# Where the row factor of the first RMSNorm is applied, how the first loads are queued, and where three transposes stand

## The chip, the cores and the metric

The kernel runs on one core of a Trainium2 chip. The time is the device time of one execution in microseconds (us). The kernel before took 1512.64, 1515.22 and 1515.03 us in three timed runs; their median is 1515.03 us. A fourth run was recorded by the hardware profiler and took 1514.31 us, of which 1512.5 us lie between its first and its last instruction. That part is called the span; 1.81 us lie around it.

Five engines work side by side, each through its own queue of instructions: PE multiplies matrices (PEld, which loads its stationary operand, runs beside it), DVE, ACT and POOL do elementwise work, and SP here only issues transfers. ACT and POOL issue some transfers too.

## The reference, cut to what matters

One layer over 256 tokens of width 2048, all in fp32:

```
u = x * rsqrt(mean(x*x) + eps) * g1           # RMSNorm
z = u @ W_in   -> stick-breaking q/k/v | forgetting q/k/v + forget logits
                  | RWKV-7 r/k/v and three low-rank inputs | 3 gates of 2048
y_A, y_B: attention (4 heads x 128 each);  y_C: RWKV-7 (16 heads x 64)
rwkv:  z = z + (z_prev - z) * mu              # shift by one token
m = sum_i sigmoid(gate_i) * (y_i @ P_i);  x = x + RMSNorm(m @ W_out)
x = x + RMSNorm(relu(RMSNorm(x) @ W_up)^2 @ W_down)
```

The factor rsqrt(...) is one number per token (a row of u), and every product with W_in is linear in u.

## The kernel before, in words

**Products.** An fp32 product is made of three faster ones. An operand is split into a high part, rounded by ACT to the matmul's format, and the rest, which DVE subtracts. Weights come from one stream of blocks of 128 x 1024 fp32 (512 KB), in the order of use, into tiles `raw` of which there are three (`wraw`, L145, issued on SP). ACT makes `whi` (L152) and DVE makes `wlo` (L153), three tiles of each; splits are made one block ahead. x or u is kept turned (features on partitions, tokens along the row) as 16 tiles of 128 x 512: 256 columns of high parts, then 256 of low parts. For a unit of 128 output columns PE multiplies whi with all 512 columns (L168, L176) and wlo with the 256 high ones (L172), eight tiles of u per block. `evac` adds the two halves of the PSUM bank (ACT copies one at L224, DVE adds at L225). A second form, `tok`, makes 256 tokens x 512 columns with u as the stationary operand (L198, L214); it serves the values of both attentions and the gates.

**Order of the work.** PE runs in the order in which its instructions are written (`manual_schedule`); on the other engines a list scheduler sets the order. The attentions and the RWKV part (`mixers`, in it `rwkv_half` for each half of the heads) and `gate_norm` are generators. They are advanced between matmuls by a virtual clock: `tick` adds 0.227 us for a matmul, `yield 3.0` holds the generator for 3.0 us of that clock, `yield "k3"` waits until `mark("k3")` is 2.6 us old (`SETTLE`).

**The begin** (L260 to L313). ACT issues the parameters and x in four pieces (L260, L263); SP issues the blocks 0, 2 and 4, then the constants. ACT and DVE split x*g1 into `xpk` (L233, L234). The first three units share the first loads: for features 0 to 7, matmuls of all three units follow as tiles arrive (L308, L310), then the products with wlo (L313); then the same for features 8 to 15 with blocks 1, 3 and 5. The fourth unit begins at L168.

**The row factor.** During unit 4, `norm` squares x, sums over features on PE (L329) and makes `rstd`, the factor per token along the row. The eight stick-breaking q and k units are made from x*g1 and scaled by DVE at L349. For everything after them, `normed` makes u = x*g1*rstd (DVE L338), splits it again (ACT L230, DVE L231) and fills the 16 tiles `upk`.

**Shift.** `shift` serves 24 r, k and v units and three low-rank inputs: ACT copies half of the bank (L525), DVE adds (L526), ACT scales by mu into a tile shifted by one token (L527), DVE combines (L528).

**The triangular inverse** in `rwkv_half` is built in `Ti` by small DVE operations (L734, L736). Then DVE turns it by a transpose into `TW` (L740) and by two into `SC` (L744), with a `yield` behind each, and PE multiplies these.

## Time and profile before

| What | Value |
|---|---|
| timed runs | 1512.64, 1515.22, 1515.03 us, median 1515.03 |
| profiled run, its span | 1514.31 us, 1512.5 us |
| PE busy | 1479.7 us, 98% |
| DVE busy | 1213.7 us, 80% |
| ACT busy | 938.4 us, 62% |
| POOL busy | 86.1 us, 6% |
| from the start to the first matmul | 8.88 us |
| first matmul of the fourth unit | 29.23 us |
| bytes moved | 317.70 MB, 210 GB/s over the span |

A row of the timeline begins with start and duration in us; then come the engine, the line of the source, the operation, the tile written, the tiles read, shapes, and the count where equal neighbours are shown as one row. The bracket at the end holds the time for which the engine had stood idle, and what released it. In the view by windows each engine has its busy us in the stretch and, in brackets, its number of instructions; the last three columns are the granted clock of PE (1.00 is full), the share of the transfer engines and GB/s. "q" behind an engine's name (SPq, ACTq) is its queue, where it issues transfers.

### The profile page before, as it was taken

How to read it: one execution, taken by the hardware profiler on the slowest of the kernel's cores; microseconds unless marked ns; L12 is line 12 of the kernel's file. 1: busy time of each engine (PE TensorE's matmuls, PEld its weight loads, DVE VectorE, ACT ScalarE, POOL GpSimd, SP SyncE). 2: the span in 40 equal slices, each digit the busy share in tenths (PEclk: the TensorE clock that was granted, in tenths of full speed). 3: DMA queues.
4: the chain of work that ended last, by engine and by line, in shares of the span. 5: the costliest groups of instructions: out<-in, count | busy, mean ns of one | idle time of the engine just before them, and what ended most of it. 6: DMA issues, size and time to landing. Idle time of an engine off the chain costs nothing.

```text
span 1512.5 us, 22758 instructions
## 1 busy us (share of the span) xinstructions
PE 1479.7 (98%) x8387; PEld 1247.3 (82%) x8387; DVE 1213.7 (80%) x1675; ACT 938.4 (62%) x1408; POOL 86.1 (6%) x159
## 2 busy tenths in 40 slices
PE   7999999999999999999999999999999999999997
PEld 6888888887777887788887888888888888888885
DVE  6876677789669799567656788999899999899996
ACT  7665666654566554565444767777677676677662
POOL 0011000100001100000000000000000000000000
PEclk9999999999999999999999999999999999999999
DMA  7555445545544445445784668888879788889884
GB/s 260 184 180 171 164 168 183 172 155 194 182 146 153 166 168 180 160 147 196 252 293 159 219 207 244 245 245 264 265 234 270 243 248 253 254 249 274 251 258 150
DMA packets 107039, 317.70 MB, mean 210 GB/s; under 512 B 10672, under 2 KB 14640, under 8 KB 106544
## 3 DMA queue, kind: packets, MB, share of 16 engines
q1 hardware_dynamic: 93536, 282.76, 54.5%
q0 software_dynamic: 8064, 29.36, 10.4%
q10 hardware_dynamic: 5328, 4.13, 0.8%
q8 instruction: 66, 1.08, 0.3%
q14 instruction: 45, 0.37, 0.1%
HBM read 282.65 MB, written 4.19 MB: 190 GB/s over the span
## 4 chain that ended last, share of the span: by engine, by line
PE 49%; issue 3%; DMA 3%; DVE 1%; ACT 0%; POOL 0%; POOLq 0%; DVEq 0%; ACTq 0%
PE gps L168 13%; PE gps L214 10%; PE gps L172 7%; PE gps L198 3%; PE mps L1324 3%; PE mps L1326 3%; PE mps L1325 3%; PE gps L1326 2%; PE gps L1324 2%; PE gps L1325 2%; PE gps L176 1%; DMA raw<-in_wst_dram 1%; DMA raw<-raw 1%; DMA sp<-raw 1%; DMA sp<-in_wst_dram 1%
## 5 line engine op out<-in xcount | busy, mean ns | idle before, releaser
L153 DVE TENSOR_TENSOR wlo<-raw,whi 128x1024 fp32r<-128x1024 f32 x507 | 616.6, 1225 | 169.4 <-ACT whi L152 155.7
L152 ACT ACTIVATE whi<-raw 128x1024 fp32r<-128x1024 f32 x507 | 532.9, 1056 | 257.1 <-DMA raw<-in_wst_dram 89.8
L168 PE MATMUL gps<-pk,whi 128*128 128x512 f32 x1301 | 330.5, 393 | 0.2 <-DVE pk L1116 0.2
L214 PE MATMUL gps<-whi,pk 128*128 128x512 f32 x1144 | 289.4, 392 | 0.0
L168 PEld LDWEIGHTS gps<-pk,whi 128*128 128x128 f32 x1301 | 241.7, 189 | 47.7 <-DVE pk L1116 0.6
L214 PEld LDWEIGHTS gps<-whi,pk 128*128 128x128 f32 x1144 | 212.7, 188 | 44.2
L172 PEld LDWEIGHTS gps<-pk,wlo 128*128 128x128 f32 x1391 | 189.9, 190 | 13.4 <-DVE wlo L153 0.2
L172 PE MATMUL gps<-pk,wlo 128*128 128x256 f32 x1391 | 195.5, 283 | 0.0
L214 PE MATMUL gps<-wlo,pk 128*128 128x512 f32 x572 | 155.6, 392 | 3.1 <-DVE wlo L153 3.1
L214 PEld LDWEIGHTS gps<-wlo,pk 128*128 128x128 f32 x572 | 106.2, 188 | 26.0 <-DVE wlo L153 3.9
L1190 DVE TENSOR_TENSOR sp<-raw,sp 128x1024 fp32r<-128x1024 f32 x67 | 81.9, 1223 | 6.6 <-ACT sp L1189 6.4
L1189 ACT ACTIVATE sp<-raw 128x1024 fp32r<-128x1024 f32 x67 | 70.5, 1053 | 15.3 <-DMA raw<-in_wst_dram 5.1
L1216 ACT ACTIVATE sp<-gps 128x512 f32<-128x512 f32 x52 | 31.0, 597 | 68.6 <-PE gps L176 68.5
L198 PE MATMUL gps<-whi,pk 128*128 128x512 f32 x264 | 72.3, 396 | 1.1 <-ACT whi L152 1.1
L1324 PE MATMUL mps<-whi,fm 128*128 128x512 f32 x168 | 66.2, 394 | 0.0
L1325 PE MATMUL mps<-whi,fm 128*128 128x512 f32 x168 | 65.9, 392 | 0.0
L1326 PE MATMUL mps<-wlo,fm 128*128 128x512 f32 x168 | 65.6, 391 | 0.0
L198 PEld LDWEIGHTS gps<-whi,pk 128*128 128x128 f32 x264 | 49.6, 190 | 12.2 <-ACT whi L152 1.8
L1286 POOL DMA_DIRECT2D raw<-raw x40 | 34.9, 873 | 428.4 <-DVE raw L1283 132.7
L1326 PE MATMUL gps<-wlo,fm 128*128 128x512 f32 x126 | 49.3, 391 | 0.4 <-DVE wlo L153 0.4
L1324 PE MATMUL gps<-whi,fm 128*128 128x512 f32 x126 | 49.3, 391 | 0.0
L1283 DVE TENSOR_TENSOR raw<-raw,raw 128x1024 f32<-128x1024 f32 x40 | 48.9, 1223 | 0.4
(383 smaller groups left out, 1984.3 us busy)
## 6 DMA issues: line engine op xcount, KB each, us to landing
raw<-in_wst_dram SPq DMA_DIRECT2D x502, 512.0 KB, 4.4
raw<-raw POOLq DMA_DIRECT2D x40, 512.0 KB, 7.5
sp<-in_wst_dram SPq DMA_DIRECT2D x16, 512.0 KB, 6.0
raw<-sp POOLq DMA_DIRECT2D x8, 512.0 KB, 7.3
sp<-raw POOLq DMA_DIRECT2D x8, 512.0 KB, 7.5
x<-in_x_dram SPq DMA_DIRECT2D x8, 256.0 KB, 6.4
xs<-x SPq DMA_DIRECT2D x2, 1024.0 KB, 4.1
x<-xs SPq DMA_DIRECT2D x4, 512.0 KB, 6.0
```

Source lines behind the costliest of these rows:

```text
L152: A.activation(hi, raw, AF.Copy)
L153: V.tensor_tensor(lo, raw, hi.bitcast(F32), ALU.subtract)
L168: PE.matmul(ps, hi[:, i * 128:i * 128 + 128], pks[i], start=first and i == 0, stop=False)
L172: PE.matmul(ps[:, 0:T], lo[:, i * 128:i * 128 + 128], pks[i][:, 0:T], start=False, stop=False)
L198: PE.matmul(ps[tt], pks[k][:, c:c + 128], w[:, (k - k0) * 512:(k - k0) * 512 + 512], start=k == 0 and part == 0 and w is hl[0], stop=w is ...
L214: PE.matmul(ps[tt], pks[k][:, c:c + 128], w[:, (k - k0) * 512:(k - k0) * 512 + 512], start=k == 0 and part == 0 and w is hl[0], stop=False)
L1189: A.activation(hi, raw, AF.Copy)
L1190: V.tensor_tensor(lo, raw, hi.bitcast(F32), ALU.subtract)
L1283: V.tensor_tensor(x, x, z, ALU.add)
L1324: PE.matmul(Q[f], p, w, start=d == 0 and i == 0, stop=False)
L1325: PE.matmul(Q[f], pl, w, start=False, stop=False)
L1326: PE.matmul(Q[f], p, wl, start=False, stop=d == nd - 1 and i == 1)
```

## The change

It has three parts.

1. **Row factor.** `normed` is gone. The 16 tiles of x*g1 that the begin makes serve all units. The factor is applied where a PSUM bank is emptied: POOL multiplies a 128 x 256 tile by `rstd` (`scaled`) for the 16 q and k units of both attentions and within the 27 shifts, between their DVE addition and ACT's scaling. Where tokens lie on partitions (`tok`), the factor goes in as the per-partition scale of the ACT instruction that empties the bank anyway: in `vtok`, and, halved, in the Tanh of the gates. `turned_rstd` makes that column form: two small matmuls turn four rows of the mean square, DVE copies, POOL raises to the power -0.5, DVE halves.
2. **Begin.** All first loads are issued on SP, in an order by need and in halves of a block. PE gets five matmuls of zeros with nothing to wait for but a memset. PE does features 0 to 3 for the three units, then 4 to 7, then 8 to 15 unit by unit. Block 1 and the last quarter of x are issued behind the other first loads; block 1 waits there for the tile `raw` of block 0. Squares are held in program order on ACT.
3. **Transposes.** `pin` (keep_in_program_order) holds the transposes into `U`, `TW` and `SC`, and a few ACT instructions, in their written place among their engine's instructions; two holds of the clock grow from 3.0 to 3.7. The tile `lor` shares the place of another one (`zx`).

The diff, cut to its core:

```diff
+    def pin(ins):
+        return tc.keep_in_program_order(ins)
...
+    zt = rp.tile([128, T], F32, tag="tha", name="zt", bufs=1)
+    V.memset(zt, 0.0)
+    idle = mps()
+    for i in range(5):
+        PE.matmul(idle[:, 0:T], zt[:, 0:128], zt, start=True, stop=True)
+    nc.sync.dma_start(out=par, in_=params)
     raws = {}
-    for a, b, n in ((0, 2, 0), (2, 4, 2), (4, 8, 4), (8, 16, 1)):
-        nc.scalar.dma_start(out=X0[:, a:b, :], in_=xt[:, a:b, :])
-        raws[n] = wraw(n)
+    def load(n, q=None):
+        if n not in raws:
+            raws[n] = wpool.tile([128, HALF], F32, tag="raw", name=nm("raw"), bufs=3)
+        cs = slice(0, HALF) if q is None else slice(512 * q, 512 * q + 512)
+        nc.sync.dma_start(out=raws[n][:, cs], in_=wst[n][:, cs])
+    def loadx(a, b):
+        nc.sync.dma_start(out=X0[:, a:b, :], in_=xt[:, a:b, :])
+    loadx(0, 2)
+    load(0, 0)
+    loadx(2, 4)
+    load(2, 0)
+    load(4, 0)
+    loadx(4, 8)
+    for n in (0, 2, 4):
+        load(n, 1)
+    loadx(8, 12)
...
-    xpk, xt2 = [], []
+    upk = []
...
     def xsplit(k):
...
+        u = pk()
         split(X0[:, k, :], u, P("g1", k))
-        xpk.append(u)
+        upk.append(u)
...
+    w = {}
+    def wpart(n, q):
+        if n not in w:
+            w[n] = (wpool.tile([128, HALF], F32R, tag="whi", name=nm("whi"), bufs=3),
+                    wpool.tile([128, HALF], F32R, tag="wlo", name=nm("wlo"), bufs=3))
+        hi, lo = w[n]
+        cs = slice(512 * q, 512 * q + 512)
+        A.activation(hi[:, cs], raws[n][:, cs], AF.Copy)
+        V.tensor_tensor(lo[:, cs], raws[n][:, cs], hi[:, cs].bitcast(F32), ALU.subtract)
+    def prods(n, ks, low):
+        for k in ks:
+            i = k % 8
+            if low:
+                PE.matmul(qb[n // 2][:, 0:T], w[n][1][:, i * 128:i * 128 + 128], upk[k][:, 0:T], start=False, stop=k == 15)
+            else:
+                PE.matmul(qb[n // 2], w[n][0][:, i * 128:i * 128 + 128], upk[k], start=k == 0, stop=False)
+    for q in range(2):
+        ks = range(4 * q, 4 * q + 4)
+        for k in ks[0:2]:
             xsplit(k)
+        wpart(0, q)
+        prods(0, ks[0:2], False)
+        for k in ks[2:4]:
+            xsplit(k)
+        prods(0, ks[2:4], False)
+        wpart(2, q)
+        prods(2, ks, False)
+        prods(0, ks, True)
+        wpart(4, q)
+        prods(4, ks, False)
+        prods(2, ks, True)
+        prods(4, ks, True)
+    load(1)
+    loadx(12, 16)
+    for n in (3, 5):
+        load(n)
+    for k in range(8, 12):
+        xsplit(k)
+    for q in range(2):
+        wpart(1, q)
+    prods(1, range(8, 12), False)
+    for k in range(12, 16):
+        xsplit(k)
+    prods(1, range(12, 16), False)
+    prods(1, range(8, 16), True)
+    for n in (3, 5):
+        for q in range(2):
+            wpart(n, q)
+        prods(n, range(8, 16), False)
+        prods(n, range(8, 16), True)
...
-    rstd = rp.tile([128, T], F32, tag="kkr", name="rstd1", bufs=1)
+    rstd = rp.tile([128, T], F32, name="rstd1")
+    rt = cpool.tile([128, 2, 4], F32, name="rt")
+    def squares(i):
+        xf = X0[:, 2 * i:2 * i + 2, :]
+        b = 2 + 2 * (i % 2) if i else 0
+        pin(A.activation(A6[:, b:b + 2, :], xf, AF.Square))
+        if i:
+            V.tensor_tensor(A6[:, 0:2, :], A6[:, 0:2, :], A6[:, b:b + 2, :], ALU.add)
...
     def norm():
-        for i in range(8):
-            xf = X0[:, 2 * i:2 * i + 2, :]
-            if i == 0:
-                A.activation(A6[:, 0:2, :], xf, AF.Square)
-            else:
-                b = 2 + 2 * (i % 2)
-                A.activation(A6[:, b:b + 2, :], xf, AF.Square)
-                V.tensor_tensor(A6[:, 0:2, :], A6[:, 0:2, :], A6[:, b:b + 2, :], ALU.add)
...
+        return ms
-    upk = [pk() for _ in range(KT)]
-    def normed(k):
-        t = tmp()
-        V.scalar_tensor_tensor(t, X0[:, k, :], P("g1", k), rstd, ALU.mult, ALU.mult)
-        split(t, upk[k])
+    def turned_rstd(ms):
+        ps = mps()
+        for tt in range(2):
+            PE.matmul(ps[:, 4 * tt:4 * tt + 4], ms[0:4, tt * 128:tt * 128 + 128], C("ident", slice(0, 4), 0, 4),
+                      start=tt == 0, stop=tt == 1)
+        r8 = rt.rearrange("p a b -> p (a b)")
+        V.tensor_copy(r8, ps[:, 0:8])
+        G.tensor_tensor(r8, r8, cst[:, 2:3].to_broadcast([128, 8]), ALU.pow)
+        V.tensor_scalar(rt[:, :, 1], rt[:, :, 0], 0.5, None, ALU.mult)
+    def scaled(d):
+        G.tensor_tensor(d, d, rstd[0:d.shape[0]], ALU.mult)
+    for i in range(2):
+        wsplit(wraw())
+        if side:
+            side.pop(0)()
+        for k in range(4 * i, 4 * i + 4):
+            squares(k)
     for h in range(8):
-        ps = qb[h] if h < 3 else unit(xpk)
+        ps = qb[h] if h < 3 else unit(upk)
...
-            norm()
+            ms = norm()
+        if h == 5:
+            turned_rstd(ms)
-            V.tensor_tensor(qk[i], qk[i], rstd, ALU.mult)
-        if h >= 3:
-            for k in range(2 * h - 6, 2 * h - 4):
-                normed(k)
-    side.extend(lambda k=k: normed(k) for k in range(10, KT))
+            scaled(qk[i])
...
+        scaled(t[0:n])
...
-        A.activation(z3[96:128], zz[96:128], AF.Copy)
+        pin(A.activation(z3[96:128], zz[96:128], AF.Copy))
...
-                lor[p] = rp.tile([128, 2, 128], F32, tag="lor", name=nm("lor"), bufs=1)
+                lor[p] = rp.tile([128, 2, 128], F32, tag="zx", name=nm("lor"), bufs=1)
...
-                A.activation(wl, raw, AF.Copy)
+                pin(A.activation(wl, raw, AF.Copy))
...
-            V.transpose(out=U[br], in_=SC[br, :, 32 * b:32 * b + 32].rearrange("s l t -> s t l"))
+            pin(V.transpose(out=U[br], in_=SC[br, :, 32 * b:32 * b + 32].rearrange("s l t -> s t l")))
...
-        V.transpose(out=TW[0:32].rearrange("t l i -> t i l"), in_=Ti[0:32].rearrange("l t i -> l i t"))
-        yield 3.0
+        pin(V.transpose(out=TW[0:32].rearrange("t l i -> t i l"), in_=Ti[0:32].rearrange("l t i -> l i t")))
+        yield 3.7
         for b in range(2):
             br = slice(32 * b, 32 * b + 32)
-            V.transpose(out=SC[br, :, 32 * b:32 * b + 32].rearrange("i l t -> i t l"), in_=Ti[br])
-            yield 3.0 if b == 0 else 4.5
+            pin(V.transpose(out=SC[br, :, 32 * b:32 * b + 32].rearrange("i l t -> i t l"), in_=Ti[br]))
+            yield 3.7 if b == 0 else 4.5
...
-            A.activation(v, ps, AF.Copy)
+            A.activation(v, ps, AF.Copy, scale=rt[:, len(vs), 0:1])
...
+            scaled(t)
...
-                A.activation(t, ps[:, i * n:i * n + n], AF.Tanh, scale=0.5)
+                A.activation(t, ps[:, i * n:i * n + n], AF.Tanh, scale=rt[:, len(ths), 1:2])
```

Three places show how instructions move. Numbers behind a name tell tiles of one name apart, and differ between the two kernels.

The queue of SP from its start: x_86 is x, raw_98, raw_101 and raw_103 are blocks 0, 2 and 4, raw_213, raw_216 and raw_218 are blocks 1, 3 and 5, and raw_312 is the first block of the fourth unit. Before (parameters and x are issued by ACT):

```order
L145 DMA raw_90<-in_wst_dram 128x1024
L145 DMA raw_93<-in_wst_dram 128x1024
L145 DMA raw_96<-in_wst_dram 128x1024
L265 DMA con<-in_consts_dram 128x1152
L266 DMA ident<-in_consts_dram 128x128
L145 DMA raw_99<-in_wst_dram 128x1024
L145 DMA raw_215<-in_wst_dram 128x1024
```

and with the change:

```order
L268 DMA par<-in_params_dram 128x116
L279 DMA x_86<-in_xt_dram 128x512
L276 DMA raw_98<-in_wst_dram 128x512
L279 DMA x_86<-in_xt_dram 128x512
L276 DMA raw_101<-in_wst_dram 128x512
...
L279 DMA x_86<-in_xt_dram 128x1024
L276 DMA raw_213<-in_wst_dram 128x1024
L279 DMA x_86<-in_xt_dram 128x1024
L276 DMA raw_216<-in_wst_dram 128x1024
L276 DMA raw_218<-in_wst_dram 128x1024
L145 DMA raw_312<-in_wst_dram 128x1024
L290 DMA con<-in_consts_dram 128x1152
```

The loads of x come into SP's queue between halves of blocks, and the constants now stand behind six blocks instead of three.

DVE at the end of the first half's inverse. Before:

```order
L740 STREAM_TRANSPOSE TW_3860<-Ti_3468 32x32x32
L153 TENSOR_TENSOR wlo_3775<-raw_3772,whi_3774 128x1024
L744 STREAM_TRANSPOSE SC_2552<-Ti_3468 32x32x32
L153 TENSOR_TENSOR wlo_3797<-raw_3794,whi_3796 128x1024
L744 STREAM_TRANSPOSE SC_2552<-Ti_3468 32x32x32
L153 TENSOR_TENSOR wlo_3825<-raw_3822,whi_3824 128x1024
```

and with the change (wlo_3763 stands for the block of wlo_3775, and so on):

```order
L153 TENSOR_TENSOR wlo_3763<-raw_3760,whi_3762 128x1024
L801 STREAM_TRANSPOSE TW_3848<-Ti_3456 32x32x32
L153 TENSOR_TENSOR wlo_3785<-raw_3782,whi_3784 128x1024
L153 TENSOR_TENSOR wlo_3813<-raw_3810,whi_3812 128x1024
L153 TENSOR_TENSOR wlo_3837<-raw_3834,whi_3836 128x1024
L153 TENSOR_TENSOR wlo_3866<-raw_3863,whi_3865 128x1024
L805 STREAM_TRANSPOSE SC_2529<-Ti_3456 32x32x32
...
L153 TENSOR_TENSOR wlo_3885<-raw_3882,whi_3884 128x1024
L153 TENSOR_TENSOR wlo_3903<-raw_3900,whi_3902 128x1024
L805 STREAM_TRANSPOSE SC_2529<-Ti_3456 32x32x32
```

Each of the three transposes comes later against the weight blocks, and at least two of the blocks' subtractions stand between one transpose and the next. In the second half, where the two transposes into SC stood side by side, one subtraction now stands between them.

ACT where `gate_norm` of the first half and `rwkv_half` of the second overlap (g, lw, tha, ep are tiles of these two, th of a gate). Before, between two weight blocks:

```order
L152 ACTIVATE whi_4883<-raw_4881 128x1024
L845 DMA gup_6651<-in_gup_dram 32x128 x2
L886 ACTIVATE g_781_4073<-g_781_4073,par 128x256
L641 ACTIVATE lw_4858<-mps_4849,wah 128x256
...
L653 ACTIVATE g_919_4901<-tha_4860,oka,wah 128x256
L976 ACTIVATE th_4912<-gps_4648 128x512
L152 ACTIVATE whi_4918<-raw_4916 128x1024
```

and with the change:

```order
L152 ACTIVATE whi_4895<-raw_4893 128x1024
L947 ACTIVATE g_756_4075<-g_756_4075,par 128x256
L906 DMA gup_6667<-in_gup_dram 32x128
L1038 ACTIVATE th_4881<-gps_4623,rt 128x512
L702 ACTIVATE lw_4860<-mps_4851,wah 128x256
L639 DMA lor_4857<-in_lora_dram 64x2x128 x2
L703 ACTIVATE tha_4862<-mps_4852,wah 128x256
...
L714 ACTIVATE g_897_4907<-tha_4862,oka,wah 128x256
L152 ACTIVATE whi_4924<-raw_4922 128x1024
```

Two issues of a transfer into lor have come between the two blocks, and one of the two into gup has gone ahead of the first. From about 640 us of the profiled execution on, the order on every engine is the same in both kernels.

29 lines of the change are left out of this document (removed).

## The prediction

> **What bounds the kernel now.** I read the page's head, then PE's list of waits, then the busy time by stretches, and the timeline only where these show a loss.
>
> ```profile
> span 1512.5 us, 22758 instructions
> ```
>
> ```profile
> PE gps L310 <- ACT whi L152: 8.9, 1, 8.9
> PE gps L214 <- DVE wlo L153: 3.1, 2, 2.0
> PE mps L1100 <- DVE x L1068: 3.0, 1, 3.0
> PE gps L198 <- DVE wlo L153: 2.4, 3, 1.1
> PE gps L198 <- ACT whi L152: 1.1, 1, 1.1
> PE gps L310 <- DVE xpk L234: 0.9, 1, 0.9
> ```
>
> Each row gives total us, number of waits and the longest. They sum to 19.4 us, and no row below them exceeds 0.5. So PE sets the time everywhere, and an edit can gain only from these waits, from PE's clock or from PE's own work. The next rows show how closed PE is between them (stretch, its length, then PE, PEld, DVE, ACT, POOL busy, clock, share of the transfer engines, GB/s):
>
> ```profile
> 8.88:15.96 7.08, 6.22 (x16) 4.56 (x16) 6.68 (x11) 6.20 (x13) 0.00 (x0) 1.00 1.03 411
> 28.00:80.00 52.00, 52.00 (x273) 44.68 (x272) 43.91 (x77) 33.12 (x53) 0.00 (x0) 1.00 0.58 196
> 130.00:360.00 230.00, 230.00 (x1358) 199.18 (x1357) 174.04 (x288) 138.01 (x229) 9.71 (x42) 1.00 0.51 172
> 462.00:487.00 25.00, 21.61 (x94) 17.01 (x92) 21.61 (x42) 15.42 (x26) 2.67 (x7) 0.93 0.46 153
> 487.00:590.00 103.00, 103.00 (x573) 85.00 (x572) 89.56 (x152) 53.21 (x79) 6.04 (x11) 1.00 0.51 172
> ```
>
> PE is busy for 52.00 of 52, 230.00 of 230 and 103.00 of 103 us. The change reaches to about 640 us. In that part PE loses time in three places only: the begin, the transposes, and 462 to 487 us. The 3.0 us at L1100 (about 822 us) lie where the order is the same in both kernels, and stay.
>
> **Term 1, the begin.** The timeline of the first 30 us:
>
> ```profile
> 0.74 1.33 SPq L145 DMA_DIRECT2D raw<-in_wst_dram  x3
> 7.37 0.51 ACT L233 ACTIVATE xpk<-x,par 128x256 fp32r<-128x256 f32 x1 [4.69 <-DMA x<-in_xt_dram]
> 7.78 1.04 ACT L152 ACTIVATE whi<-raw 128x1024 fp32r<-128x1024 f32 x1
> 8.86 1.22 DVE L153 TENSOR_TENSOR wlo<-raw,whi 128x1024 fp32r<-128x1024 f32 x1 [0.46 <-ACT whi L152]
> 8.88 0.80 PE L310 MATMUL gps<-xpk,whi 128*128 128x512 f32 x1 [8.88 <-ACT whi L152]
> 12.83 1.91 PE L310 MATMUL gps<-xpk,whi 128*128 128x512 f32 x4
> 14.54 1.58 PE L308 MATMUL gps<-xpk,whi 128*128 128x512 f32 x5
> 18.02 3.04 PE L313 MATMUL gps<-xpk,wlo 128*128 128x256 f32 x24
> 29.23 2.00 PE L168 MATMUL gps<-xpk,whi 128*128 128x512 f32 x8
> 34.83 1.03 PE L329 MATMUL mps<-a,con 128*128 128x256 f32 x4
> ```
>
> ```profile
> raw<-in_wst_dram SPq DMA_DIRECT2D x10, 512.0 KB, 4.4
> x<-in_xt_dram ACTq DMA_DIRECT2D x2, 256.0 KB, 6.9
> par<-in_params_dram ACTq DMA_DIRECT2D x1, 58.0 KB, 4.1
> ```
>
> The first matmul stands behind the first piece of x (6.9 us from issue to landing), ACT's split of it (0.5) and of a whole block (1.04), and starts at 8.88. The transfers then run at 411 GB/s, all at once. Four matmuls take 14.54 - 12.83 = 1.71 us, 0.43 each, where eight later take about 1.82 (29.23 on, 0.227 each): PE runs at half rate until about 15 us, though the clock column shows 1.00 there. A product with wlo takes 3.04 / 24, about 0.12.
>
> After: the transfers come in one line, so the first 570 KB (parameters, two tiles of x, half a block) no longer share with 2 MB. At 411 GB/s they take 1.4 us instead of being spread; I put their landing between 4.2 and 5.1 us (the parameters landed 4.1 after their issue at 0.74). One split of x (0.5) and of half a block (about 0.6, half of 1.04 and something fixed) put the first matmul near 6.0. The idle matmuls, ten passes at the 0.26 of L329 or at twice that, end between 3.8 and 6.4, so they delay it by 0.4 at most.
>
> From there the splits pace the work: features 0 to 7 are eight of 0.5 and six of 0.6, 7.6 us on ACT and as much on DVE, so DVE is done with block 0 at about 10.6 and PE with this half at about 13 to 15.2. Block 1 waits for that tile: 10.6 + 4.4 = 15.0. ACT splits it by 16.2. The last four tiles of x, issued behind it, land at 15.0 + 1.3 (512 KB at 411 GB/s); four splits on ACT and DVE bring the last to 19.1. Behind it PE has 0.23, 8 x 0.12 and two blocks of 8 x (0.227 + 0.12): 6.75, so 25.9 for the fourth unit instead of 29.23.
>
> Between about 15.2 and 19.1 PE has then only 1.8 us of work. In the trace two idle times of 1.1 us close to each other are followed by a slow stretch:
>
> ```profile
> 473.75 1.07 PE L198 MATMUL gps<-whi,pk 128*128 128x512 f32 x4
> 480.52 1.19 PE L198 MATMUL gps<-whi,pk 128*128 128x512 f32 x4 [1.15 <-ACT whi L152]
> 482.84 1.22 PE L198 MATMUL gps<-wlo,pk 128*128 128x512 f32 x2 [1.13 <-DVE wlo L153]
> 483.86 1.91 PE L198 MATMUL gps<-whi,pk 128*128 128x512 f32 x4
> ```
>
> Four matmuls take 1.91 instead of 1.07 there; the stretch lasts from 482.84 to about 486.2 and loses half of it, 1.7 us. The rows do not tell whether the begin would meet this; I count half, 0.85. Term 1 is 25.9 + 0.85 - 29.23 = **-2.5**. Best end: block 1 never ends last, PE runs on from 15.2 with 24 x 0.347 = 8.3 and is done at 23.5, -5.7. Worst: block 1 takes the 6.9 of the crowded x and the clock falls, 25.9 + 2.5 + 1.7 = 30.1, +0.9.
>
> The Trainium skill, page "TensorE: Matmul & The Clock Gate", section "The HAM clock gate (the 'warmup' mystery)", says that PE starts at half rate, gets the full rate after a busy window of about 3.4 us, and falls back after an idle one, the window running free of the program. The half rate to about 15 us agrees; the slow stretch at 482.84 does not, since PE had worked there within any 3.4 us. By the rule the begin would keep its clock between 15.2 and 19.1, and term 1 would be -3.3.
>
> **Term 2, the transposes.**
>
> ```profile
> 369.23 2.13 DVE L740 STREAM_TRANSPOSE TW<-Ti 32x1024 f32<-32x1024 f32 x1
> 371.25 1.17 DVE L153 TENSOR_TENSOR wlo<-raw,whi 128x1024 fp32r<-128x1024 f32 x1
> 372.35 2.01 DVE L744 STREAM_TRANSPOSE SC<-Ti 32x1024 f32<-32x1024 f32 x1
> 593.51 4.00 DVE L744 STREAM_TRANSPOSE SC<-Ti 32x1024 f32<-32x1024 f32 x2
> ```
>
> ```profile
> 372.48 0.73 PE L198 MATMUL gps<-wlo,pk 128*128 128x512 f32 x2 [0.69 <-DVE wlo L153]
> 378.80 0.73 PE L198 MATMUL gps<-wlo,pk 128*128 128x512 f32 x2 [0.58 <-DVE wlo L153]
> 598.82 1.20 PE L214 MATMUL gps<-wlo,pk 128*128 128x512 f32 x4 [1.99 <-DVE wlo L153]
> ```
>
> Three waits, 0.69 + 0.58 + 1.99 = 3.26. Each time DVE stood in one or two transposes of 2.0 while PE used up its one block ahead. PE takes 2.7 us for a block (12 matmuls of 0.227), DVE 1.2 for its wlo. A transpose and a wlo, 3.3, lag by 0.6 behind PE's block; two blocks between transposes regain 3.0. In the first half the new order has four and two wlos between transposes, so no lag remains. In the second half there is one wlo between neighbours: three transposes and their wlos, 9.7 us, stand against three blocks of 8.2, a lag of 1.5 that one block ahead (2.7) can carry. I take **-3.3**; the bounds are -3.3 and, if the lag is met in the second half, -1.8.
>
> **Term 3, work of PE.** `turned_rstd` adds two matmuls with a moving tile of four columns. The nearest row, L329, gives 0.26 for a pass over 256 columns; two passes each bound it by 1.0, and below by nothing. At the full rate 512 columns take 0.227 and 256 take 0.12 in the rows above, so time goes with columns, and four are nearer the lower end; with something for the change of operands: **+0.3**.
>
> **Term 4, 462 to 487 us.** PE waits there three times for about 1.1 us and loses 1.7 to its clock. ACT's order shows ten or more small instructions and issues between two blocks; the change puts two issues into lor among them and moves one into gup ahead. This speaks for a longer wait; that DVE's inverse ends later by a block or two speaks for either. Ends: all three waits and the slow clock go, -5.1; or ACT stays away longer by two issues of 0.4 (1.33 / 3 at the start), each met twice, and by a second slow stretch, +3.4. The order moves little of what stands there, so I take a value near nothing, on the side of the added issues: **+1.0**.
>
> **Term 5, what moves to POOL, and what is gone.**
>
> ```profile
> L661 POOL TENSOR_TENSOR Bt<-kkr,ep 128x256 f32<-128x256 f32 x8 | 6.0, 752 | 2.7 <-DVE kkr L656 2.7
> ```
>
> ```profile
> L338 DVE SCALAR_TENSOR_TENSOR tmp<-x,par,rstd 128x256 f32<-128x256 f32 x16 | 7.4, 487 | 0.0
> ```
>
> `normed` goes: 16 instructions of 0.487 on DVE, with its splits about 15 us of DVE and 7 of ACT. It lies in 28 to 80 us, where PE is busy for 52.00 of 52. PE covered it all, so its end gives 0. Sixteen scalings move from DVE to POOL by the same argument for 0; the scale of ACT in `vtok` and the gates adds no instruction. The 27 shifts get 0.75 us each on POOL in the chain from bank to result. DVE idles for 56 of 230 us there, ACT for 92 and POOL for 220, and the result is needed only 2.6 us of virtual clock after the mark; an instruction on ACT or DVE that stands behind a late POOL result delays a block's split by less than a block's slack of 1.5 us. Cover gone, it is 0.75 a shift. I take **+0.4**, bounds 0 and +2.
>
> **Sum.** -2.5 - 3.3 + 0.3 + 1.0 + 0.4 = -4.1. Against the profiled run of 1514.31 us that is 1510.2. The median of the runs is 0.7 above the profiled run and the lowest run 1.7 below it; I forecast 1510.4.
>
> **Rivals.** A change within 0.2% (1512.0 to 1518.1) can't be told from none by a measurement of this kernel.
>
> - Forecast: all terms near their values. Adding bounds that are unlikely together only in part (-1.6 and +2 for the begin, 1.5 for the transposes, 2 for the rest): 1507 to 1513. Chance 0.60.
> - Larger gain: the moved order also dissolves the waits of 462 to 487. Term 4 becomes -5.1, the begin -3.3: 1514.3 - 3.3 - 3.3 - 5.1 + 0.7 = 1503.3. For it: those waits hang on single places in the queues, and everything there shifts. Against it: ACT's order keeps its lump. Chance 0.08.
> - The lump grows: term 4 at +3.4, 1512.6. For it: two issues more between two blocks. Against: the waits may be taken by others that shrink. Chance 0.14.
> - The begin gives nothing, since block 1 ends last and the clock falls: term 1 at +0.9, the sum -0.7, 1513.6. For it: block 1 is issued at 10.6, while before it was issued near 10 as well. Against: the first matmul 2.9 us earlier, and full rate sooner. Chance 0.11.
> - Slower: POOL's factor ends last in the shifts. ACT's scaling waits for POOL, and behind it in ACT's queue stands the next block's whi, which PE needs. 27 x 0.75 = 20 us, 1510.2 + 20 = 1530; above 1518.1 from 7.9 / 27 = 0.29 us a shift on. Against it the slack above. Chance 0.07.
>
> What DVE loses while POOL works is seen at 96.9 to 103.8 us, where POOL runs without a pause: wlo takes 1353 ns there and 1222 in the 16 us behind it.
>
> ```profile
> L153 DVE TENSOR_TENSOR wlo<-raw,whi 128x1024 fp32r<-128x1024 f32 x3 | 4.0, 1353 | 0.0
> L153 DVE TENSOR_TENSOR wlo<-raw,whi 128x1024 fp32r<-128x1024 f32 x8 | 9.8, 1222 | 2.5 <-ACT whi L152 2.5
> ```
>
> That is a tenth of POOL's time, 0.08 us a shift, below what decides. The Trainium skill, page "SBUF — State Buffer", section "SBUF: two separate sides", has a DVE instruction with two SBUF inputs wait out the whole of a POOL instruction. By that rule a shift would cost DVE 0.75, against its 56 us of idle; the row of 1353 does not bear the rule out.
>
> **How the numbers follow.** Outside 1505 to 1515 lie the slower rival, the larger gain and a small part of the rest, 2 in 10; the forecast's own range is 1507 to 1513. Faster by over 0.2% (below 1512.0): 0.52 of the forecast's 0.60, the 0.08, and a half of what the lump and the begin leave by their spread, 0.08: 0.68. Slower: the POOL rival, 0.07. The rest, 0.25, is within 0.2%.
>
> **What would show it.** The begin: first matmul near 6.0 and the fourth unit's at about 26; a clock below 1.00 near 20 would show the fall. Transposes: no wait for wlo of over 0.2 us beside L801 and L805. POOL: PE busy for all of the stretch from 130 to 360 us; a wait for zp or whi there would show the last rival. 462 to 487: three waits of about 1.1 us, moved by little. Everything behind 640 us should be only shifted. I am wrong if PE waits in the shifts, or if the begin ends later than 28.

## The result: slower by half a per cent

The changed kernel took 1522.25 us (median of five runs, 1518.15 to 1523.12), the kernel before 1512.64 beside it (five runs, 1511.99 to 1515.22). The ratio, estimated from all runs, is 1.0052, with a 95% interval of 1.0034 to 1.0070 (the two medians alone would give 1.0064); 0.0052 are 7.9 us. I had forecast 1510.4 with 0.07 for slower. The profiled run of the changed kernel took 1523.08 us. One execution of the kernel y3 below took 3415.1 us, more than twice the others, and counts in none of its figures.

Head of the page, changed kernel:

```profile
span 1521.3 us, 22774 instructions
PE 1489.9 (98%) x8401; PEld 1253.3 (82%) x8401; DVE 1210.3 (80%) x1644; ACT 937.7 (62%) x1398; POOL 139.2 (9%) x203
```

PE's waits, changed kernel (total us, number, longest):

```profile
PE mps L696 <- DVE lows L647: 6.3, 2, 3.3
PE gps L198 <- DVE wlo L153: 2.3, 1, 2.3
PE gps L168 <- ACT whi L152: 2.1, 1, 2.1
PE mps L378 <- DVE a L373: 2.1, 1, 2.1
PE mps L1162 <- DVE x L1130: 1.9, 1, 1.9
PE gps L328 <- DVE pk L237: 1.8, 1, 1.8
PE mps L267 <- DVE zt L264: 1.2, 1, 1.2
```

The wait of 8.9 us at the start is gone, and so are the three behind the transposes. In their place stand waits that the kernel before does not have: for `lows` (the split of the low-rank weights), for a weight block at 107 us, for the sum of squares. PE's busy time, too, has grown by 10 us at nearly the same number of matmuls: the ten passes of zeros at the start hold PE for 4.6 us, and more of the others ran at half rate.

Where the time came from is best read as a ledger. From the fourth unit on, both kernels work through the same weight blocks, so the start of a block's first matmul in one timeline minus that in the other is the lead or lag so far. The table gives what each stretch adds (us, by the times of the kernel before; plus is time lost against it), for the changed kernel and for the experiments that follow:

| kernel | to 29 | 29–58 | 58–109 | 109–246 | 246–268 | 268–362 | 362–388 | 388–467 | 467–504 | 504–604 | 604–1498 |
|---|---|---|---|---|---|---|---|---|---|---|---|
| changed | -2.4 | 3.0 | 3.9 | -0.1 | 6.1 | 2.5 | -1.6 | 0.7 | 1.8 | -2.3 | -2.6 |
| x1 split not held | -2.8 | 2.2 | 2.4 | 0.3 | 0.0 | 3.8 | -1.6 | 0.7 | -2.8 | -2.3 | -1.0 |
| x2 factor on DVE | -2.7 | 2.9 | 0.8 | -0.1 | 3.7 | 0.1 | -1.9 | 0.7 | 2.6 | -2.3 | -1.9 |
| x3 squares later | -2.4 | 0.7 | 4.0 | -0.1 | 6.3 | 2.6 | -1.5 | 0.7 | 1.8 | -2.3 | -0.3 |
| x4 transposes alone | 0.4 | 0.0 | 0.0 | 0.0 | 0.0 | 0.0 | -1.9 | 0.6 | -2.8 | -2.3 | 2.4 |
| y1 begin alone | -2.5 | 1.3 | 0.0 | 0.0 | 0.0 | 0.1 | 0.1 | 0.0 | -1.6 | 1.6 | -0.5 |
| z1 held split alone | 0.6 | 0.8 | 0.0 | 0.0 | 1.5 | 0.0 | -0.1 | 0.0 | 1.7 | -0.4 | -3.6 |
| y2 three mends, DVE | -2.7 | 0.7 | 0.8 | -0.1 | 0.0 | 0.1 | -1.9 | 0.7 | -1.6 | -2.3 | -3.9 |
| y4 the same, POOL | -2.9 | 0.7 | 2.4 | 0.8 | 0.0 | 3.2 | -1.6 | 0.7 | -1.6 | -2.3 | -3.2 |
| z2 q, k on POOL | -2.7 | 0.7 | 1.2 | -0.1 | 0.0 | 0.1 | -1.9 | 0.7 | -2.9 | -2.3 | -3.8 |
| z4 shifts on POOL | -2.8 | 0.7 | 0.6 | 0.7 | 0.0 | 3.8 | -1.6 | 0.7 | -2.8 | -2.3 | -3.4 |

The last column is the long part in which the orders are alike; it varies by several us from one execution to the next (in x4, a wait of 2.3 us and a slow stretch at 1316 us that no other execution has), so single-profile differences there mean nothing. The first column scatters too: x4 and z1, whose begin is that of the kernel before, show 0.4 and 0.6 there. The row of the changed kernel adds up to 9.0; its span is 8.8 longer. y3 and z3 are left out of the table: y3 reads like x4 with a begin of -1.6 and 0.8 lost at 29–58, z3 like y2 but for the last column (-1.1).

**The begin.** Timeline of the changed kernel:

```profile
5.71 0.95 PE L328 MATMUL gps<-pk,whi 128*128 128x512 f32 x2
26.83 2.00 PE L168 MATMUL gps<-pk,whi 128*128 128x512 f32 x8
31.94 0.62 ACT L371 ACTIVATE a<-x 128x512 f32<-128x512 f32 x1
33.90 0.68 DVE L373 TENSOR_TENSOR a<-a 128x512 f32<-128x512 f32 x1
34.64 1.13 PE L378 MATMUL mps<-a,con 128*128 128x256 f32 x4 [2.06 <-DVE a L373]
```

The first matmul starts at 5.71 and the fourth unit at 26.83 instead of 29.23. But the sums of squares are ready no sooner than they were: ACT's last square ends at 32.56, DVE's last addition at 34.58 (33.71 in the kernel before), and PE, which now arrives earlier, waits 2.06 us. The gain is given back 8 us after it was made.

**At 107 us.** The same timeline:

```profile
102.36 0.74 POOL L395 TENSOR_TENSOR g<-g,rstd 128x256 f32<-128x256 f32 x1
103.06 2.48 POOL L448 TENSOR_TENSOR sbt<-sbt,con 128x128 f32<-128x128 f32 x4
105.57 0.84 ACT L454 ACTIVATE sbh<-sbt 128x768 fp32r<-128x768 f32 x1 [2.30 <-POOL sbt L448]
106.59 1.99 ACT L152 ACTIVATE whi<-raw 128x1024 fp32r<-128x1024 f32 x2
107.69 3.00 PE L168 MATMUL gps<-pk,whi 128*128 128x512 f32 x8 [2.12 <-ACT whi L152]
```

A factor (L395) stands on POOL ahead of the multiplications by the mask (L448); ACT waits for those at L454, and behind L454 in ACT's queue stands the weight split whi, for which PE waits. The eight matmuls then take 3.00 us instead of 2.00.

**At 263 us.** The same timeline; L645 and L647 make the split of the low-rank weights, L588 and L589 are ACT's and DVE's last steps of a shift:

```profile
258.80 0.41 ACT L645 ACTIVATE lows<-lor 128x256 fp32r<-128x256 f32 x1
260.00 0.83 POOL L395 TENSOR_TENSOR tmp<-tmp,rstd 128x256 f32<-128x256 f32 x1 [2.60 <-DVE tmp L586]
260.87 0.51 ACT L588 ACTIVATE zp<-tmp,par 128x256 f32<-128x256 f32 x1 [1.67 <-POOL tmp L395]
262.44 0.47 DVE L589 SCALAR_TENSOR_TENSOR g<-tmp,omu,zp 128x256 f32<-128x256 f32 x1
262.95 0.60 DVE L647 TENSOR_TENSOR lows<-lor,lows 64x128 fp32r<-64x128 f32 x2
263.38 0.98 PE L696 MATMUL mps<-lows 128*128 128x256 f32 x3 [3.33 <-DVE lows L647]
```

In the kernel before the same split was done long ahead of its use:

```profile
30.80 0.42 ACT L584 ACTIVATE lows<-lor 128x256 fp32r<-128x256 f32 x1
34.76 0.28 DVE L586 TENSOR_TENSOR lows<-lor,lows 64x128 fp32r<-64x128 f32 x1
255.38 0.52 PE L635 MATMUL mps<-lows 128*128 128x256 f32 x3
```

The source writes this split just ahead of the matmuls that use it. The scheduler had moved it forward to 30.80; the change holds ACT's half of it in its written place, so it runs at 258.80, and its DVE half stands behind a shift that waits for POOL. The same happens in the second half of the heads (490.76 us):

```profile
484.46 0.40 ACT L645 ACTIVATE lows<-lor 128x256 fp32r<-128x256 f32 x1
490.32 0.29 DVE L647 TENSOR_TENSOR lows<-lor,lows 64x128 fp32r<-64x128 f32 x1
490.76 1.14 PE L696 MATMUL mps<-lows 128*128 128x256 f32 x3 [2.95 <-DVE lows L647]
```

### The profile page after: what moved, and what is told of

Read it like the earlier page. It is cut to its first block, busy times and chain, and to the rows that moved or that the text cites. A ratio compares the mean times of both kernels' runs of the same rounds, so it can differ in the third digit from the quotient of the medians.

```text
span 1521.3 us, 22774 instructions
## 1 busy us (share of the span) xinstructions
PE 1489.9 (98%) x8401; PEld 1253.3 (82%) x8401; DVE 1210.3 (80%) x1644; ACT 937.7 (62%) x1398; POOL 139.2 (9%) x203
## 4 chain that ended last, share of the span: by engine, by line
PE 64%; DVE 2%; issue 1%; DMA 1%; ACT 1%; POOL 0%; POOLq 0%; DVEq 0%; ACTq 0%
PE gps L214 18%; PE gps L168 14%; PE gps L172 8%; PE gps L198 5%; PE mps L1386 3%; PE mps L1388 3%; PE mps L1387 3%; PE gps L1388 2%; PE gps L1386 2%; PE gps L1387 2%; PE gps L176 1%; DVE wlo L153 1%; DMA sp<-in_wst_dram 1%; PE mps L745 0%; ACT whi L152 0%
## 5 line engine op out<-in xcount | busy, mean ns | idle before, releaser
L152 ACT ACTIVATE whi<-raw 128x1024 fp32r<-128x1024 f32 x501 | 527.1, 1056 | 251.9 <-PE gps L214 113.1
L168 PE MATMUL gps<-pk,whi 128*128 128x512 f32 x1366 | 348.2, 394 | 2.2 <-ACT whi L152 2.1
L168 PEld LDWEIGHTS gps<-pk,whi 128*128 128x128 f32 x1366 | 254.2, 190 | 52.6 <-ACT whi L152 2.4
L172 PEld LDWEIGHTS gps<-pk,wlo 128*128 128x128 f32 x1456 | 200.3, 192 | 14.4 <-DVE wlo L153 0.2
L172 PE MATMUL gps<-pk,wlo 128*128 128x256 f32 x1456 | 205.4, 284 | 0.0
```

The source lines that it names most:

```text
L152: A.activation(hi, raw, AF.Copy)
L168: PE.matmul(ps, hi[:, i * 128:i * 128 + 128], pks[i], start=first and i == 0, stop=False)
L172: PE.matmul(ps[:, 0:T], lo[:, i * 128:i * 128 + 128], pks[i][:, 0:T], start=False, stop=False)
```

## The experiments

Each kernel was timed beside the kernel before on the same chip; the ratio is to that kernel, with its 95% interval. The kernel before took 1513.72 us (median) beside the x runs, 1515.16 beside the y runs and 1513.68 beside the z runs, so runs of different letters are compared by their ratios. The columns named are those of the table above.

### One cause mended at a time

**x1: the low-rank split not held.**

```diff
-                pin(A.activation(wl, raw, AF.Copy))
+                A.activation(wl, raw, AF.Copy)
```

> The changed kernel with one edit: the split of the low-rank weights on ACT (wl) is no longer held in its written place, so the scheduler may do it as soon as its load is there, as before. Theory A (the held split is late: PE waits 3.3 us at 263 and 2.9 at 491 for lows, and the slow clock after each costs 1.7 to 3.4 more): both waits for lows go, the time falls by about 6 at the first place and 2 to 5 at the second, so about 1510 to 1514 us instead of 1522. Theory B (POOL's factor, which stands in front of the split in DVE's chain there, is what is late): the waits move to another instruction and the time stays within 2 us of 1522.

Measured: 1515.17 us, ratio 1.0010 (0.9999 to 1.0021), where the changed kernel has 1.0052: 0.0042, or 6.4 us. Both waits for `lows` are gone; the split runs at 185.04:

```profile
185.04 0.40 ACT L645 ACTIVATE lows<-lor 128x256 fp32r<-128x256 f32 x1
```

In the ledger 246–268 falls from 6.1 to 0.0 and 467–504 from 1.8 to -2.8. Theory A holds in its mechanism; the gain is smaller than the 8 to 11 us that it gave. In the ledger the two places give back 10.7 and 268–362 takes 1.3 more; a ledger compares one execution of each kernel, and the ratio of all runs shows 6.4.

**x2: the factor on DVE.**

```diff
-        G.tensor_tensor(d, d, rstd[0:d.shape[0]], ALU.mult)
+        V.tensor_tensor(d, d, rstd[0:d.shape[0]], ALU.mult)
```

> The changed kernel with one edit: the 43 multiplications by the row factor run on DVE instead of POOL. Theory B (POOL's operation, 0.74 us alone and up to 2.0 beside DVE, ends last): the wait of 2.1 us at 107 and its slow clock go (3.9 us), and the waits for lows at 263 shrinks by what POOL adds there, 1 to 3 us; 1515 to 1518 us. Theory A: the wait at 107 goes, those for lows stay at 3.3 and 2.9; 1518 to 1519. If POOL doesn't matter at all: 1520 to 1524, DVE having 18 us more work.

Measured: 1515.74 us, 1.0012 (0.9995 to 1.0029), 6 us below the changed kernel. 58–109 falls from 3.9 to 0.8, 246–268 from 6.1 to 3.7, 268–362 from 2.5 to 0.1. Both theories hold a part: POOL costs time at three places, and the held split still makes PE wait:

```profile
PE mps L696 <- DVE lows L647: 4.9, 2, 3.0
```

DVE's 43 added instructions cost at most the 0.8 that stays at 58–109, where PE waits 0.4 for a weight split; y3 below, which does not have them, loses nothing in that stretch.

**x3: the sums of squares one unit later.**

```diff
-        if h == 3:
+        if h == 4:
             ms = norm()
...
-        for i in range(h + 1) if h == 3 else [h] if h > 3 else []:
+        for i in range(h + 1) if h == 4 else [h] if h > 4 else []:
```

> The changed kernel with one edit: PE multiplies the sums of squares one unit (6 us of PE) later. Theory: the begin is 2.4 us shorter, but the sums of squares end when they did, so PE waits 2.1 us for them at 34.6 and gives the gain back. Then this wait goes and nothing takes its place before 100 us: 1520 us, 2.1 to 2.3 below the changed kernel. If squares are slow for another reason (held in order behind the constants), the wait is found again one unit later with 2 us or less, and the time stays at 1522.

Measured: 1519.42 us, 1.0037 (1.0024 to 1.0050), against 1.0052. The wait at L378 is gone and the stretch 29–58 falls from 3.0 to 0.7. The 2.3 us are as expected in the ledger; by the ratios the step is 0.0015 and inside the intervals.

### One part of the change alone

**x4: the transposes.** The kernel before with

```diff
-        V.transpose(out=TW[0:32].rearrange("t l i -> t i l"), in_=Ti[0:32].rearrange("l t i -> l i t"))
-        yield 3.0
+        pin(V.transpose(out=TW[0:32].rearrange("t l i -> t i l"), in_=Ti[0:32].rearrange("l t i -> l i t")))
+        yield 3.7
...
-            V.transpose(out=SC[br, :, 32 * b:32 * b + 32].rearrange("i l t -> i t l"), in_=Ti[br])
-            yield 3.0 if b == 0 else 4.5
+            pin(V.transpose(out=SC[br, :, 32 * b:32 * b + 32].rearrange("i l t -> i t l"), in_=Ti[br]))
+            yield 3.7 if b == 0 else 4.5
```

and the same `pin` at the transposes into U.

> The kernel before with the third part of the change alone: the transposes into U, TW and SC held in their written place and the two holds of 3.7. If this part does what term 2 said, the waits of 0.69, 0.58 and 1.99 us at 372, 379 and 599 go and nothing else moves: 1509 to 1510.5 us against 1512.6. If the scheduler shifts what stands behind it into new waits (as the 462 to 487 stretch), 1511 to 1515.

Measured: 1509.16 us, 0.9969 (0.9956 to 0.9982), 4.6 us faster. The waits at 372, 379 and 599 are gone (-1.9 and -2.3). And 467–504 gains 2.8, which neither line expected: the three waits of 1.1 us there have become one, and no slow clock follows it.

```profile
474.00 0.74 PE L198 MATMUL gps<-wlo,pk 128*128 128x512 f32 x2 [2.38 <-DVE wlo L153]
```

**y1: the begin.** The kernel before with the loads, the idle matmuls, the order of the first three units and the squares of the changed kernel; `normed`, the scaling on DVE, the transposes and the low-rank split as before.

> The kernel before with the second part of the change alone: loads in one queue and in halves, idle matmuls, the new order of the first three units, squares held in order; the row factor is applied as before and the transposes stand as before. Theory (the sums of squares are the next thing late): the fourth unit starts at 26.5 to 27 instead of 29.2, PE waits 1 to 2.3 us at the sum of squares near 34, and the time is that of the kernel before within 1.5 us. Rival (the wait came with the row factor's other work): no wait there, 2.4 us below the kernel before.

Measured: 1511.32 us, 0.9974 (0.9959 to 0.9990). The fourth unit starts 2.5 us earlier. Between 29 and 58 us 1.3 of them are lost, 0.6 of it a wait at the sum of squares. So neither line is right: the squares take back a part, not all, and 1.2 us stay. The wait is 0.63 here and 2.06 in the changed kernel, and ACT begins the squares at 22.58 here and at 24.11 there; whether the row factor's work or the chance of one execution makes this difference was not tried. The whole row sums to -1.5 us, 0.9990, which is the upper end of the interval; where the ratio's other 2.4 us would be, one profile does not tell.

**z1: the held split.** The kernel before with

```diff
-                A.activation(wl, raw, AF.Copy)
+                pin(A.activation(wl, raw, AF.Copy))
```

> The kernel before with one edit: the ACT split of the low-rank weights is held in its written place. Nothing else of the change is there: factor, begin and transposes are as before. Theory A (the held split alone makes PE wait): PE waits for lows at the first matmul of both halves, 1 to 3 us each, with 1.7 to 3.4 of slow clock where the wait fills half a window of the clock: 3 to 9 us above the kernel before, 1.002 to 1.006 of it. Theory B (it is late only because POOL's factor stood in the chain ahead of it): within 1.5 us of the kernel before.

Measured: 1516.77 us, 1.0030 (1.0017 to 1.0043), 4.5 us slower with POOL's factor nowhere in the kernel. Theory A holds:

```profile
PE mps L638 <- DVE lows L589: 4.5, 2, 3.4
```

This one line makes a kernel slower by itself without adding an instruction. The other ACT copy that the change holds, and the place that `lor` shares, were not tried alone; y2 below has both and no wait for `lows`.

### The causes together, and the price of POOL

**y2: three mends** (x1, x2 and x3 in one kernel).

> The changed kernel with three edits: split of the low-rank weights not held, the row factor on DVE, sums of squares one unit later. If the three causes found apart add up (6 for the held split, 5 to 6 for POOL, 2.3 for the squares), PE has the begin's -2.5, the turned factor's +0.7, the transposes' -1.9 and -2.3 and no new wait: 5 to 8 us below the kernel before, 0.995 to 0.9965 of it. If any reordering brings new waits of its own (scheduler's chance), it stays within 2 us of the kernel before.

Measured: 1504.75 us, 0.9940 (0.9919 to 0.9962): 9 us faster than the kernel before, a little more than the 5 to 8 expected, and 17 us (0.0112) faster than the changed one. One at a time the three gave 0.0042, 0.0040 and 0.0015, in sum 0.0097: within the intervals they add up. PE is busy without a gap from 110 to 360 us and from 480 to 590:

```profile
110.00:360.00 250.00, 250.00 (x1475) 216.77 (x1474) 200.24 (x342) 151.94 (x248) 16.18 (x51) 1.00 0.55 176
480.00:590.00 110.00, 110.00 (x604) 90.76 (x603) 96.94 (x163) 58.79 (x85) 11.57 (x13) 1.00 0.54 177
```

**y3: begin and transposes, without the row factor's move.** The kernel before with the second part, the transposes of the third (its two held ACT copies and the shared place of `lor` are not in it), and the sums of squares one unit later; u is made again by `normed`.

> The kernel before with the second and third part of the change, sums of squares one unit later, and the row factor as before (u made again by DVE and ACT). Theory: removing that work gained nothing, since PE covered it; so this gains the begin's 2.5 and what the transposes alone gained (0.9969 of the kernel before, 4.6 us): 0.995 to 0.9955, 6 to 7.5 us below. If the removed work had been worth something, it is slower than the changed kernel with its three causes mended.

Measured: 1507.97 us (median of four), 0.9953 (0.9935 to 0.9972). Against y2's 0.9940, 2 us less, the intervals overlap widely: whether the removed 15 us of DVE work and 7 of ACT are worth anything can't be told. In the ledger each has a small loss of its own. With the shorter begin y3's PE waits 0.56 us for a weight block at 55.95 while u is made, which y2 does not; y2 has the turned factor and the 0.8 at 58–109 instead.

**y4: two mends, factor on POOL** (x1 and x3).

> The changed kernel with two edits: split of the low-rank weights not held, sums of squares one unit later; the row factor stays on POOL. Against the same with the factor on DVE this prices POOL: the wait of 2.1 us at 107 (with or without 1.7 of slow clock) and 2 to 3 us between 300 and 345: 4 to 6 us slower than that kernel, 0.999 to 1.000 of the kernel before. If POOL doesn't matter once the split is early, the two agree within 1 us.

Measured: 1512.46 us, 0.9985 (0.9975 to 0.9995). Against y2 that is 0.0045, 6.8 us, a little more than expected: the price of putting the factor on POOL. The ledger has it at 58–109 (2.4 for 0.8), 109–246 (0.8 for -0.1) and 268–362 (3.2 for 0.1).

**z2: only the 16 q and k factors on POOL; z4: only the 27 of the shifts**, both from y2.

```diff
-    def scaled(d):
-        V.tensor_tensor(d, d, rstd[0:d.shape[0]], ALU.mult)
+    def scaled(d, e=None):
+        (e or V).tensor_tensor(d, d, rstd[0:d.shape[0]], ALU.mult)
```

with `G` given by the q and k units in z2 and by `shift` in z4.

> The kernel with the three mends, but the 16 multiplications of the q and k units back on POOL, those of the shifts on DVE. Theory: they stand between the POOL multiplications by the mask at 96 to 107 us, and ACT, queued ahead of a weight split, waits for those: the wait of 2.1 us at 107 comes back (0.4 there with DVE), 1.5 to 3.5 us above the three mends, and nothing is lost behind 110 us. If the loss at 107 has another cause: same as the three mends within 1 us.

> The kernel with the three mends, but the 27 multiplications of the shifts back on POOL, those of q and k on DVE. Theory: POOL's operation takes 0.74 us alone and 1.6 to 2.0 when it starts beside a DVE operation with two SBUF operands, and makes that operation longer when it starts first; in 27 chains this costs 3 to 5 us between 140 and 350 us and nothing at 107. If only the q and k factors mattered: same as the three mends within 1 us.

Measured: z2 1504.18 us, 0.9935 (0.9919 to 0.9951), the same as y2; z4 1509.58 us, 0.9965 (0.9952 to 0.9978), 0.0025 or 3.8 us slower than y2. The intervals of z4 and y2 overlap; those of z4 and z2, timed side by side, do not (0.0030 apart). The shifts cost what was expected (3.8 at 268–362). The q and k factors did not cost what was expected: alone on POOL they add 0.4 at 58–109 and nothing to the time. So my reading of the wait at 107 us, a factor ahead of the masks, is not enough. With both kinds on POOL it is there (changed kernel, x1, y4: 2.1 us), with either kind alone it is not (0.6 or less). The orders of POOL and ACT around it differ among these kernels, and which difference decides was not tried.

**z3: y2 without the five idle matmuls** and their memset.

> The kernel with the three mends, without the memset and the five idle matmuls. By the traces PE is at half rate for 3.4 us from about 9 us on in spite of them, and waits for splits around it, so they are worth 0 to 1 us. If they keep the clock up from 6 to 9 us and the next splits aren't in the way, up to 2 us are lost without them.

Measured: 1506.57 us, 0.9948 (0.9933 to 0.9963); not to be told from y2. The first matmul on data starts at 6.60 there and at 7.11 in y2, the fourth unit at 26.48 and 26.54. In z3:

```profile
6.60 4.04 PE L323 MATMUL gps<-pk,whi 128*128 128x512 f32 x8 [6.60 <-ACT whi L314]
26.48 2.00 PE L168 MATMUL gps<-pk,whi 128*128 128x512 f32 x8
```

What PE waits for at the begin of y2 are splits (1.4 us for whi and 0.4 for a tile of x); the idle matmuls are worth nothing here that can be told.

## Why the prediction was wrong

The forecast was -4.1 us and the measured change +7.9. Three steps failed: the held split had no term (6.4 us), POOL's term of +0.4 was 6.8, and nothing was counted for what PE would wait for next behind the shorter begin (2.3).

**Term 1 (the begin, -2.5): right in size, and its gain not kept.** The first matmul on data came at 5.71 (6.0 forecast), the fourth unit at 26.83 (26.7). What failed is the step behind it: I priced the begin up to the fourth unit and did not ask what would be late next. It was the sum of squares, whose work on ACT and DVE the begin does not shorten: 2.06 us of waiting, in the ledger 2.3 (x3), and 0.63 of waiting with the begin alone (y1).

**Term 2 (the transposes, -3.3): right.** -1.6 and -2.3 in the changed kernel, -1.9 and -2.3 alone (x4); the waits at 372, 379 and 599 are gone. Some 0.7 comes back at 388–467 in every kernel that holds the transposes and in neither y1 nor z1, so that -3.2 to -3.5 stay. Where it comes from was not followed.

**Term 3 (the turned factor, +0.3): 0.7** (29–58 in x3 and y2).

**Term 4 (462 to 487 us, +1.0): +1.8, and near it by luck.** I looked at two issues into `lor` among ACT's instructions. The transposes alone make this stretch 2.8 faster (x4), and x1, without the held split, is as fast there. The held split adds 4.6 to it; the two happen to leave a sum near mine.

**What no term held: the held split.** It cost 6.4 us in the changed kernel (x1) and 4.5 by itself (z1), and is, with POOL's, the largest loss. The part of the text on the change named "a few ACT instructions" held in place, and the prediction gave them no line, though the trace showed their split done at 30.80 and used at 255.38. Holding this instruction in its written place took back what the scheduler had moved forward; its lead could be read in the trace of before.

**Term 5 (POOL, +0.4): 6.8 us** (y4 against y2), 3.8 of it in the shifts (z4). This is the rival to which I gave 0.07, with up to 20 us in the shifts. Its mechanism (ACT waits for POOL, and behind that in ACT's queue stands the weight split for which PE waits) is what the rows at 107 us show, though there ACT waits for the masks and not for a shift. In the shifts it is not what PE waits for. In z4, from 262 to 365 us, PE waits for small results of the RWKV part, made by DVE and ACT among the shifts, and once for wlo, but never for whi; y2 has none of these waits:

```profile
PE mps L771 <- DVE SC L755: 0.5, 1, 0.5
PE mps L745 <- DVE At L723: 0.5, 1, 0.5
PE gps L214 <- DVE wlo L153: 0.3, 1, 0.3
PE mps L771 <- ACT Kt L758: 0.2, 1, 0.2
PE mps L752 <- DVE kpl L735: 0.2, 1, 0.2
```

The waits sum to 1.7 us; how they become the 3.8 of the ledger was not worked out. So the first wrong step is the slack: 1.5 us is what a weight block can be late, and I held it against results for which it says nothing. The second is the sentence "the row of 1353 does not bear the rule out". That row was a mean over three instructions of which two met POOL, and it looked at DVE's side only. POOL's side stood in the same trace of before; shortest, median and longest of its eight multiplications there are, in ns:

```profile
L388 POOL TENSOR_TENSOR sbt<-sbt,con x8: 456/834/1442, 96.9 to 102.6; 128x128 f32<-128x128 f32 x8
```

The two of 1.44 us (at 97.33 and 98.73) are those that start beside a running split of DVE. The trace of the changed kernel shows both sides. POOL first, and DVE's split of a block takes 1.76 instead of 1.22:

```profile
214.91 0.73 POOL L395 TENSOR_TENSOR tmp<-tmp,rstd 128x256 f32<-128x256 f32 x1 [2.53 <-DVE tmp L586]
214.95 1.76 DVE L153 TENSOR_TENSOR wlo<-raw,whi 128x1024 fp32r<-128x1024 f32 x1
```

DVE first, and POOL's multiplication takes 1.65 instead of 0.74:

```profile
110.82 1.21 DVE L153 TENSOR_TENSOR wlo<-raw,whi 128x1024 fp32r<-128x1024 f32 x1
110.98 1.65 POOL L395 TENSOR_TENSOR g<-g,rstd 128x256 f32<-128x256 f32 x1 [1.50 <-DVE g L228]
```

Each is lengthened by most of what the other still had to run: DVE by 0.54 where POOL had 0.69 left, POOL by 0.91 where DVE had 1.05 left. Over the changed kernel the factor in the shifts took 1190 ns in the mean, not 752:

```profile
L395 POOL TENSOR_TENSOR tmp<-tmp,rstd 128x256 f32<-128x256 f32 x26 | 30.9, 1190 | 111.2 <-DVE tmp L586 105.0 <-DVE foxsm L549 6.2
```

The Trainium skill says this, on the page "SBUF — State Buffer" in the section "SBUF: two separate sides": a DVE instruction with two SBUF inputs and a POOL instruction that reads SBUF exclude each other for a whole instruction, whichever starts first. The rows above agree to within 0.15 us. Which one comes first can't be read off the records where they start close together: at 254.20 POOL's record starts 0.18 ahead of DVE's split, and it is POOL that takes 1.98 and the split that takes 1.21. I had set the rule aside for a mean that could not refute it. No run separates what the lengthening costs from what the added 0.74 us in the chain would cost without it.

**Slow clock.** The waits above cost more than their length. Windows of the changed kernel around the wait at 107 and that at 263:

```profile
105.20:108.60 3.40, 1.28 (x7) 0.84 (x6) 2.15 (x3) 3.03 (x5) 1.12 (x2) 1.00 0.00 0
108.60:112.00 3.40, 3.40 (x14) 2.90 (x13) 3.40 (x4) 2.03 (x4) 1.90 (x2) 0.50 0.56 166
258.80:262.20 3.40, 1.25 (x9) 0.82 (x7) 3.37 (x6) 1.73 (x4) 0.83 (x1) 1.00 0.44 167
262.20:265.60 3.40, 2.22 (x7) 2.02 (x8) 2.42 (x5) 0.78 (x3) 0.10 (x1) 0.50 0.47 166
265.60:269.00 3.40, 3.40 (x13) 3.03 (x12) 0.69 (x1) 0.70 (x3) 0.00 (x0) 0.50 0.58 186
```

At 263 a wait of 3.3 us is followed by 6.8 us at half rate; together they are the 6.1 us of that stretch. In x1 a wait of 2.1 us at the same place as the one at 107 has no slow clock behind it: it falls across two windows.

```profile
102.40:105.80 3.40, 1.94 (x13) 1.50 (x11) 1.75 (x3) 1.46 (x3) 1.91 (x3) 1.00 0.21 84
105.80:109.20 3.40, 2.75 (x15) 2.41 (x16) 3.40 (x4) 3.36 (x6) 1.67 (x1) 1.00 0.17 34
```

That is the difference between 3.9 and 2.4 us in the table's third column. My term 1 counted half a slow stretch behind 15 us; one came from 9.6 us on instead, so that term 1 came out near its size is in part luck.

## What to carry to other kernels

Before an instruction is held in its written place, read from the trace how long ahead of its use it ran: that lead is what the holding takes away, and whatever stands before the written place can then make it late. When a change makes an engine arrive earlier, price the next thing it will wait for, and take as covered only what is still covered at the new time. Work put on POOL beside DVE instructions with two SBUF operands is to be priced as its own time plus what is left of the other's, on both engines, and against every result behind the chain that it stands in, not the weight splits alone; a mean over a window does not show it.

## What the runs showed of the hardware

- The granted clock changes on a grid of 3.41 us: in every profile here half rate lasts 3.4 us or a multiple (but for the last stretch, which the end cuts off), and its starts within one execution are whole multiples of that apart (in the changed kernel 9.63, 108.62, 262.22 and 487.50 us: 29, 74 and 140 windows behind the first). Over the fourteen profiles and behind the first 10 us, a window at full rate of which PE was idle for a share of 0.60 or more (by the modelled ends of its matmuls) was followed by half rate in all 27 cases; below a share of 0.38 none was, and between them 16 of 32 were. The rows above show two: 1.28 us busy of 3.40 at 105.20 in the changed kernel, with half rate behind it, and 1.94 of 3.40 at 102.40 in x1, without. So a wait of some 2 us costs 1.7 more, or nothing, by where it falls. The Trainium skill, page "TensorE: Matmul & The Clock Gate", section "The HAM clock gate (the 'warmup' mystery)", has the window and that it runs free of the program; that a window need not be idle in whole, and that a share of 0.60 was always enough, is what these runs add.
- The clock column shows 1.00 ahead of its first recorded change. In z3 it does so while eight matmuls take 4.04 us, 0.5 each, against 2.00 for eight at 26.48. Spacing, not the column, tells the rate there.
